# mLSTM loads and mixer stores on GpSimd's DMA queue, and a second buffer for a head's queries

## The chip, the cores and the metric

One core of a Trainium2 chip runs one program. The metric is device time in microseconds for one execution; the kernel before has a median of 1392.73 us over three runs (1391.56 to 1393.49). Five engines work side by side, each through its own instructions in order: TensorE (PE, with its weight loads as PEld), VectorE (DVE), ScalarE (ACT), GpSimd (POOL) and SyncE (SP). SP does no arithmetic here: it issues nearly all DMA transfers. POOL does arithmetic and can issue transfers too; in the profile these lie on a queue of their own kind ("software_dynamic", q0), SP's on q1 ("hardware_dynamic").

## The reference: what is computed

One transformer-like layer over two groups of rows, 1024 prompt rows and 32 sample rows, 1024 features each, all in float32:

```python
h = x * (1 + sc1) + sh1                      # adaLN, from silu(c) @ w_ada
mq, mk, mv, mo, mi, mf, fq, fk, fv, ff, gu, gv = split(h @ w_in)
hm = head_norm(mlstm(mq, mk / 8, mv, li, lf)) * g * sigmoid(mo)      # 4 heads of 64, chunked
hf = softmax_causal(fq @ fk.T / 8 + Fi - Fj) @ fv                    # 8 heads of 64, "FoX"
hg = gu * (tril(ws) @ layer_norm(gv) + bs)                           # gMLP, 4 groups
mix = concat([hm, hf, hg]) @ w_o
x = layer_norm(ALPHA * x + (1 + g1) * mix)
y = (silu(h2 @ w_gate) * (h2 @ w_up)) @ w_down                       # h2 = x * (1 + sc2) + sh2
x = layer_norm(ALPHA * x + (1 + g2) * y)
```

The mLSTM goes over the rows chunk by chunk with a matrix state C that each chunk updates; the FoX heads are causal softmax attention. New keys, values, gates and states are outputs too.

## The kernel before

**Numbers.** Each float32 product is made of three float32r products: every operand is split into a high and a low part (`whi`, `wlo`, `h1h`, `h1l`, `qkh`, `qkl`), and `gemm` issues high x high, high x low, low x high (lines 117 to 119).

**Order.** The kernel is written for a scheduler that orders each engine's instructions by a timeline simulation when the program is built. The source gives the rough order, priorities and buffer counts; the order inside an engine is the scheduler's. Tiles come from pools; a tag with one buffer means that the next tile of that tag waits until all readers of the last one are done.

**Phase one** (some 160 to 360 us in the profile) holds the projections and half of the mixing. The string `ORDER` interleaves units of the input projection (`q0` to `q7`: one FoX head's queries and keys; `k0`, `k1`, `v`, `o`: the mLSTM's; `a`: a piece of the adaLN product) with the mixers of the first 512 rows: `f0` to `f7` are `self.fox(i, ((0, 1, 2, 3),))`, `m0` to `m3` are `self.mlstm(i)`, both at a raised priority. Projections leave SBUF for DRAM scratch (`dqh`, `dql`, `dv`, `dmqk`, `dmv`, `dmo`), and the mixers load them again.

A call of `fox` issues nine loads for a head: the queries `qp` (two) and `q2` (two), the keys `k1` (two) and `k2` (two), and `v`. The tuple `foxbufs` gives the buffers of `k1`, of the queries (`qp` and `q2` together), of `k2`, of `v`, and of the transposed probabilities. In phase one it is (2, 1, 1, 2, 3). For each block of 128 queries `fox_chunk` makes the scores with two matmuls (lines 702 and 703: `qp` with `k1`, then `q2` with `k2`), the row maximum on DVE, the exponential on ACT (line 711) and the scaling on DVE (line 719); then come transposes (738), products with `v` (746, 751), and the end: ACT copies the upper half of the result to `fo` (758), DVE adds it to the lower half into `fr` (759), and `fr` is stored to `dmix`, the scratch that holds the concatenated mix, feature-major.

A call of `mlstm` handles 128 rows. It issues six loads (`mqk`, two for `mqb`, `mv`, `mo`, `mb`), all tags with one buffer; POOL clears `mqb` (525) and sets a column of `mv` (530) before their loads. ACT then makes a sigmoid of `mo` (538 to 540), POOL scales it (541), PE makes the scores (552), products (568, 573) and the new state (583), and DVE normalises (603 to 621). `to_mix` transposes the result on PE (631), ACT copies it to `mixs` (633), and a store takes it to `dmix`. `to_mix` serves the gMLP as well, with `k0=6` in place of 0.

**After phase one** the gMLP units run (`gv` with POOL's scaling in lines 353 and 354, then `gu` with `evac_gmlp`; in two of the four units POOL also makes `wlo`, line 106). The pools of phase one are closed, and the memory goes to `ph`, `pz` and `p2`: `wo_res` loads the residual (tile `z0`, seen in the profile as `mlstm_z<-xT`), `wo_mix` loads the mix from `dmix` (`wo_tmp`), and `wo` multiplies by `w_o`.

**The second half of the rows** is mixed in `mixers` (some 480 to 880 us), with another pool and `foxbufs` (2, 1, 1, 1, 2): each head takes two chunks of two tiles, woven with `mlstm(4)` to `mlstm(8)`, while the first group's feed-forward products fill PE. The rest is the second `wo` and the feed-forward of the second group.

`load` and `store` both issue on SP:

```python
    def load(self, out, in_):
        self.lastload = self.nc.sync.dma_start(out, in_)
        return self.lastload
```

## Time and profile before

| | |
|---|---|
| median of three runs | 1392.73 us (1391.56 to 1393.49) |
| the profiled execution | 1390.37 us, span 1388.5 us |
| PE busy | 1345.2 us, 97% of the span |
| DVE, ACT, POOL busy | 1034.2, 641.3, 259.1 us |
| DMA on SP's queue | 221.34 MB, 50.7% of the 16 engines |
| DMA on POOL's queue | 9.96 MB, 4.7% (all of it from line 1057, late in the kernel) |
| granted TensorE clock, mean | 0.993 |

A busy PE in these rows is not a PE at its peak: matmul ends are modelled. What tells of lost time is PE's idle time and what ended it. Idle time of the other engines costs nothing unless PE comes to wait for it.

### The profile page before, as it was taken

To read this page: it belongs to the slowest core of one execution; us is meant where nothing else is said; L and a number is where in the kernel's file an instruction comes from. 1 tells how busy PE (TensorE), PEld (TensorE's weight loads), DVE (VectorE), ACT (ScalarE), POOL (GpSimd) and SP (SyncE) were. 2 spreads that over 40 slices of the span, in tenths; PEclk is the share of its full clock that TensorE was granted. 3 is DMA by queue.
4 is the path that set the end of the run, shared out by engine and by line. 5 is a ranking of instruction groups with operands and counts; after the bars stand their busy time and mean duration, and the time that the engine had idled before them with its cause. 6 is when DMAs were issued, how large, how long until landed. Compare 5 with 4: busy or idle time off the path is not lost.

```text
span 1388.5 us, 25995 instructions
## 1 busy us (share of the span) xinstructions
PE 1345.2 (97%) x9683; PEld 1236.4 (89%) x9683; DVE 1034.2 (74%) x2214; ACT 641.3 (46%) x1261; POOL 259.1 (19%) x292
## 2 busy tenths in 40 slices
PE   7999999999999799999999999999999999999996
PEld 4899988899899778888887889899999999999996
DVE  5548656678689657777776766677898988888777
ACT  3323234444455444545544445335574544545355
POOL 0103200052157500000000000264610000000341
PEclk9999999999999899999999999999999999999998
DMA  9754577575665665444443442664497767453321
GB/s 362 266 211 134 176 242 212 187 237 149 212 205 160 180 184 182 125 131 137 133 135 86 108 127 81 195 169 134 157 229 195 216 163 214 136 175 115 101 90 65
DMA packets 136373, 233.09 MB, mean 168 GB/s; under 512 B 22564, under 2 KB 79532, under 8 KB 136248
## 3 DMA queue, kind: packets, MB, share of 16 engines
q1 hardware_dynamic: 130936, 221.34, 50.7%
q0 software_dynamic: 5168, 9.96, 4.7%
q8 instruction: 76, 1.25, 0.4%
q14 instruction: 49, 0.40, 0.1%
q10 hardware_dynamic: 144, 0.14, 0.0%
HBM read 197.50 MB, written 53.81 MB: 181 GB/s over the span
## 4 chain that ended last, share of the span: by engine, by line
PE 67%; DVE 5%; DMA 3%; ACT 1%; issue 1%; SPq 0%; POOL 0%; DVEq 0%; ACTq 0%
PE up_g L117 5%; PE up_g L118 5%; PE up_g L119 5%; PE dn_g L119 4%; PE dn_g L117 4%; PE dn_g L118 4%; PE sup_u L119 3%; PE sup_u L117 3%; PE sup_u L118 3%; PE wo_g L119 2%; PE wo_g L117 2%; PE wo_g L118 2%; PE sup_g L118 2%; PE sup_g L119 2%; PE sup_g L117 2%; PE fox_t L738 2%
## 5 line engine op out<-in xcount | busy, mean ns | idle before, releaser
L117 PE MATMUL up_g<-mlstm_ah,up_whi 128*128 128x512 f32 (+1 forms) x384 | 141.7, 369 | 4.4 <-ACT lna_tmp L981 3.3
L118 PE MATMUL up_g<-mlstm_al,up_whi 128*128 128x512 f32 (+1 forms) x384 | 142.1, 370 | 0.4 <-DVE mlstm_al L986 0.4
L119 PE MATMUL up_g<-mlstm_ah,up_wlo 128*128 128x512 f32 (+1 forms) x384 | 141.1, 368 | 0.0
L282 PE MATMUL tm_g<-tm_whi,start_h1h 128*128 128x256 f32 (+1 forms) x384 | 109.7, 287 | 1.5 <-ACT tm_mixs L633 1.5
L284 PE MATMUL tm_g<-tm_whi,start_h1l 128*128 128x256 f32 (+1 forms) x384 | 109.6, 287 | 0.0
L283 PE MATMUL tm_g<-tm_wlo,start_h1h 128*128 128x256 f32 (+1 forms) x384 | 109.5, 286 | 0.0
L117 PE MATMUL fm_g<-start_h1h,fm_whi 128*128 128x256 f32 (+2 forms) x344 | 101.7, 301 | 6.1 <-DVE fm_qkl L367 2.6
L118 PE MATMUL fm_g<-start_h1l,fm_whi 128*128 128x256 f32 (+2 forms) x344 | 100.8, 293 | 0.0
L119 PE MATMUL fm_g<-start_h1h,fm_wlo 128*128 128x256 f32 (+2 forms) x344 | 100.0, 292 | 0.0
L1105 ACT CAST sup_whi<-sup_raw 128x1024 fp32r<-128x1024 f32 x54 | 56.0, 1048 | 91.5 <-PE dn_u L118 47.9
L117 PEld LDWEIGHTS up_g<-mlstm_ah,up_whi 128*128 128x128 f32 x384 | 73.5, 192 | 16.7 <-ACT mlstm_ah L985 3.5
L118 PEld LDWEIGHTS up_g<-mlstm_al,up_whi 128*128 128x128 f32 x384 | 73.7, 192 | 12.3 <-DVE mlstm_al L986 1.5
L119 PEld LDWEIGHTS up_g<-mlstm_ah,up_wlo 128*128 128x128 f32 x384 | 73.8, 192 | 10.6
L105 ACT CAST up_whi<-up_raw 128x1024 fp32r<-128x1024 f32 x50 | 52.4, 1048 | 63.9 <-PE dn_g L118 25.1
L711 ACT ACTIVATE fox_p<-fox_s,fox_fmx 128x384 f32<-128x384 f32 (+2 forms) x96 | 55.0, 578 | 57.1 <-DVE fox_fmx L709 44.0
L282 PEld LDWEIGHTS tm_g<-tm_whi,start_h1h 128*128 128x128 f32 x384 | 72.2, 189 | 4.4 <-ACT tm_mixs L633 2.1
L117 PEld LDWEIGHTS fm_g<-start_h1h,fm_whi 128*128 128x128 f32 x344 | 64.7, 190 | 12.5 <-DVE fm_qkl L367 3.5
L1106 DVE TENSOR_TENSOR sup_wlo<-sup_raw,sup_whi 128x1024 fp32r<-128x1024 f32 x54 | 67.8, 1259 | 10.5 <-ACT sup_whi L1105 10.5
L106 DVE TENSOR_TENSOR up_wlo<-up_raw,up_whi 128x1024 fp32r<-128x1024 f32 x50 | 66.8, 1336 | 10.4 <-ACT up_whi L105 9.6
L284 PEld LDWEIGHTS tm_g<-tm_whi,start_h1l 128*128 128x128 f32 x384 | 72.2, 188 | 1.5 <-issue 1.2
L117 PE MATMUL dn_g<-up_acth,dn_whi 128*128 128x512 f32 (+2 forms) x200 | 73.5, 368 | 0.0
L118 PE MATMUL dn_g<-up_actl,dn_whi 128*128 128x512 f32 (+2 forms) x200 | 73.3, 368 | 0.0
(591 smaller groups left out, 4594.5 us busy)
## 6 DMA issues: line engine op xcount, KB each, us to landing
up_raw<-w_gu SPq DMA_DIRECT2D x50, 512.0 KB
dn_raw<-w_dn SPq DMA_DIRECT2D x28, 512.0 KB
ada_late<-w_ada SPq DMA_DIRECT2D x24, 512.0 KB
wo_raw<-w_o SPq DMA_DIRECT2D x24, 512.0 KB
sup_raw<-w_gu SPq DMA_DIRECT2D x20, 512.0 KB
start_dp<-w_gu SPq DMA_DIRECT2D x19, 512.0 KB
start_dp<-w_gu POOLq DMA_DIRECT2D x19, 512.0 KB, 7.8
sup_raw<-start_dp SPq DMA_DIRECT2D x18, 512.0 KB
```

Source lines behind the costliest of these rows:

```text
L105: nc.scalar.copy(hi[:, :w], raw[:, :w])
L106: (eng or nc.vector).tensor_tensor(lo[:, :w], raw[:, :w], f(hi[:, :w]), ALU.subtract)
L117: nc.tensor.matmul(ps, hi, xh(k), start=start and k == 0, stop=False)
L118: nc.tensor.matmul(ps, hi, xl(k), start=False, stop=False)
L119: nc.tensor.matmul(ps, lo, xh(k), start=False, stop=stop and k == n - 1)
L282: nc.tensor.matmul(ps[:, :ncol], xh, hi, start=k == 0, stop=False)
L283: nc.tensor.matmul(ps[:, :ncol], xh, lo, start=False, stop=False)
L284: nc.tensor.matmul(ps[:, :ncol], xl, hi, start=False, stop=k == 7)
L711: nc.scalar.activation(pr[:, lo:hi], banks[x][:, :hi - lo], AF.Exp, bias=mxs[:, 0:1], accum_out=sums[:, x:x + 1])
L738: nc.tensor.transpose(ps[:, c:c + P], probs[y][:, b * P:(b + 1) * P], self.ident)
L1105: nc.scalar.copy(h, x)
L1106: tt(l, x, f(h), ALU.subtract)
```

## The change

All six loads of `mlstm` are issued on GpSimd in place of SP (nine calls, 54 transfers). The mLSTM's store in `to_mix` goes to GpSimd (nine), the gMLP's stays on SP. The end of a FoX chunk adds in place into `fo`, the tile `fr` is gone, and its store goes to GpSimd (8 in phase one, 16 in `mixers`). In phase one the queries `qp` and `q2` get two buffers each.

```diff
         qk = t([P, 4, P], "mqk", 1)
-        self.load(qk[:, :, :L], self.dmqk[:, :, o:o + L])
+        self.nc.gpsimd.dma_start(qk[:, :, :L], self.dmqk[:, :, o:o + L])
         qb = t([P, 2, 2, P], "mqb")
         nc.gpsimd.memset(qb, 0.0)
         for a in range(2):
             r = slice(64 * a, 64 * a + 64)
-            self.load(qb[r, :, a, :L], self.dmqk[r, 0:2, o:o + L])
+            self.nc.gpsimd.dma_start(qb[r, :, a, :L], self.dmqk[r, 0:2, o:o + L])
         v = t([P, 4, 65], "mv1", 1)
         nc.gpsimd.memset(v[:, :, 64:65], 1.0)
-        self.load(v[:L, :, 0:64], self.dmv[:L, j, :].rearrange("p (h e) -> p h e", h=4))
+        self.nc.gpsimd.dma_start(v[:L, :, 0:64], self.dmv[:L, j, :].rearrange("p (h e) -> p h e", h=4))
         mo = t([P, 256], "mo", 1)
-        self.load(mo[:L], self.dmo[:L, j, :])
+        self.nc.gpsimd.dma_start(mo[:L], self.dmo[:L, j, :])
         mb = t([P, 4, P], "mb", 1)
-        self.load(mb[:L, :, :L], self.dM[:, j, :L].partition_broadcast(L))
+        self.nc.gpsimd.dma_start(mb[:L, :, :L], self.dM[:, j, :L].partition_broadcast(L))
...
-        self.store(self.dmix[c][:, k0:k0 + 2, o:o + L], s[:, :, :L])
+        (nc.sync if k0 else nc.gpsimd).dma_start(self.dmix[c][:, k0:k0 + 2, o:o + L], s[:, :, :L])
...
         tmp = t([64, nq], F32, "fo", 1)
-        r = t([64, nq], F32, "fr", 1)
         nc.scalar.copy(tmp[:, :nq], o[64:128, :nq])
+        r = tmp
         nc.vector.tensor_tensor(r[:, :nq], o[0:64, :nq], tmp[:, :nq], ALU.add)
         c = tiles[0] // 4
         o = tiles[0] * P - GO[c]
-        self.store(self.dmix[c][64 * (h % 2):64 * (h % 2) + 64, 2 + h // 2, o:o + nq], r[:, :nq])
+        nc.gpsimd.dma_start(self.dmix[c][64 * (h % 2):64 * (h % 2) + 64, 2 + h // 2, o:o + nq], r[:, :nq])
...
-        self.foxbufs = (2, 1, 1, 2, 3)
+        self.foxbufs = (2, 2, 1, 2, 3)
```

## The prediction

> **What bounds the kernel now.** I read the page's totals first, then the busy time by stretches, then who waited for whom on PE between 155 and 400 us, then the instructions of SP, PE, ACT and POOL around the waits found.

> ```profile
> span 1388.5 us, 25995 instructions
> PE 1345.2 (97%) x9683; PEld 1236.4 (89%) x9683; DVE 1034.2 (74%) x2214; ACT 641.3 (46%) x1261; POOL 259.1 (19%) x292
> ```

> PE is the bound; time is won only where PE stands idle. The stretches (us; busy time of PE, PEld, DVE, ACT, POOL, then the granted clock, the DMA share and GB/s) say where that is in reach of this change:

> ```profile
> 160.00:200.00 40.00, 39.77 (x328) 35.04 (x326) 17.91 (x56) 13.77 (x37) 2.04 (x4) 1.00 0.87 263
> 200.00:240.00 40.00, 38.58 (x323) 34.30 (x321) 24.06 (x58) 17.97 (x42) 2.95 (x4) 1.00 0.71 203
> 240.00:280.00 40.00, 38.35 (x320) 34.85 (x313) 25.18 (x74) 17.76 (x46) 2.09 (x4) 1.00 0.61 194
> 280.00:320.00 40.00, 38.11 (x316) 36.25 (x315) 29.86 (x92) 16.40 (x40) 16.78 (x17) 1.00 0.79 235
> 320.00:360.00 40.00, 38.95 (x329) 37.27 (x327) 35.69 (x120) 17.81 (x49) 14.39 (x15) 1.00 0.40 120
> 360.00:400.00 40.00, 35.94 (x289) 34.30 (x288) 25.06 (x54) 20.02 (x43) 8.12 (x11) 1.00 0.80 248
> 480.00:880.00 400.00, 398.93 (x2159) 331.07 (x2152) 284.64 (x610) 195.13 (x394) 9.85 (x15) 1.00 0.45 131
> ```

> Phase one (160 to 360) has 0.23 + 1.42 + 1.65 + 1.89 + 1.05 = 6.2 us of idle PE, the passage to `wo` (360 to 400) 4.1 us, and the 400 us in which the second half is mixed only 1.1 us, though most of the moved transfers lie there. What this change can win is thus a few microseconds of phase one. The waits of PE there, with total, times and longest:

> ```profile
> PE fox_s L702 <- DMA fox_qp<-start_dql: 3.3, 4, 1.6
> PE fox_s L702 <- issue: 0.7, 1, 0.7
> PE fox_s L703 <- DMA fox_k<-start_dql: 0.2, 1, 0.2
> ```

> These are the first score matmuls of a head, waiting for its queries. The one row "issue" has no releaser; I count it with them, as it stands at the same matmul. That is 4.0 us for line 702 and 0.2 us for line 703.

> **Part 1: two query buffers, and fewer transfers ahead of them on SP.** The longest of these waits, with what SP did ahead of it:

> ```profile
> 247.80 0.79 SPq L91 DMA_DIRECT2D start_dmix<-fox_fr  x1
> 248.69 0.55 SPq L87 DMA_DIRECT2D fox_qp<-start_dqh  x1
> 249.28 0.59 SPq L87 DMA_DIRECT2D fox_qp<-start_dql  x1
> 249.92 0.59 SPq L87 DMA_DIRECT2D fox_q<-start_dqh  x1
> 250.56 0.48 SPq L87 DMA_DIRECT2D fox_q<-start_dfs  x1
> 251.08 0.45 SPq L87 DMA_DIRECT2D fox_k<-start_dql  x1
> 251.57 0.48 SPq L87 DMA_DIRECT2D fox_k<-start_dfs  x1
> 253.04 0.47 PE L702 MATMUL fox_s<-fox_k,fox_qp 128*128 128x128 f32 x2 [1.65 <-DMA fox_qp<-start_dql]
> ```

> All six loads have single buffers, freed by the last head's last score matmul; they leave SP one after another, behind a head's store. With a second buffer the four query loads can go a head earlier, and only the two of `k2` still wait. Then 0.45 + 0.48 = 0.93 us of issues stand where 0.55 + 0.59 + 0.59 + 0.48 + 0.45 + 0.48 = 3.14 us stood, so `k2` leaves 2.2 us earlier, and 3.0 us with the store (0.79) gone from SP. The 4.0 us of line 702 go; the 0.2 us of line 703, late next, stay or go. I take -4.0 us, with the ends -4.2 us and 0 (if the scheduler doesn't move the loads forward, or moves the head forward with them, so that `k2` becomes the wait).

> [...]

> **Part 2: the stage from 480 to 880 us.** ACT runs in order, and a late `mo` holds what stands behind it:

> ```profile
> 739.51 0.31 SPq L87 DMA_DIRECT2D mlstm_mo<-start_dmo  x1
> 746.09 0.42 ACT L538 ACTIVATE mlstm_mo<-mlstm_mo 32x256 f32<-32x256 f32 x1 [4.76 <-DMA mlstm_mo<-start_dmo]
> 748.57 0.45 PE L702 MATMUL fox_s<-fox_k,fox_qp 128*128 128x384 f32 x1 [0.51 <-ACT fox_p L711]
> ```

> The load took 6.6 us from issue to use and cost PE 0.51 us. Whether POOL's queue brings it sooner no row shows. The ends are -1.1 us (all the idle time of the stage) and +2.5 us (five calls, each 0.51 us again); I take -0.5 us, since weights no longer stand ahead of this load on its own queue. Moving the other loads and 16 stores off SP wins nothing there: PE hides them.

> **Part 3: the store that ends phase one.** The chain of waits from 360 us on:

> ```profile
> 360.96 0.38 SPq L91 DMA_DIRECT2D start_dmix<-mlstm_mixs  x1
> 362.56 3.75 SPq L87 DMA_DIRECT2D mlstm_z<-xT  x8
> 366.35 5.20 DMA wo_tmp<-start_dmix
> ```

> The last mLSTM's store frees the memory into which the eight residual loads go, behind which the loads of the mix stand, and `wo` behind those. The store is now issued by POOL, whose only transfers so far are these (minimum, median, maximum in ns; then us to landing; then the sizes, the moved store's too):

> ```profile
> L1057 POOL DMA_DIRECT2D start_dp<-w_gu x19: 1026/1035/1533, 926.8 to 1227.2; - x19
> DMA to landing us min/median/max: 6.1/7.8/11.6
> start_dp<-w_gu POOLq DMA_DIRECT2D x19, 512.0 KB, 7.8
> start_dmix<-mlstm_mixs SPq DMA_DIRECT2D x8, 128.0 KB
> ```

> An issue takes 1.035 us on POOL against 0.38 us on SP, 0.65 us more. At the far end, a landing of 7.8 us in place of at most 1.6 us (360.96 to 362.56) is +6.2 us; but that row is of 512 KB, four times this store's 128 KB. I take +1.0 us, near the issue's difference, and charge all of it, as PE already waits in this stretch.

> **Part 4: POOL's time.** There are 54 + 9 + 24 = 87 new transfers, 87 x 1.035 = 90 us on an engine busy for 259.1 us of 1388.5. Some 36 lie in phase one (24 loads, 4 and 8 stores), 37 us, where POOL is busy for 38.3 of 200 us. On that queue stand the products of line 541, the key sums of line 368, the gMLP's scaling (353, 354) and two units' `wlo` (106). I cost that at nothing on the path: PE runs on accumulation banks filled ahead. What it costs without this cover is rival two.

> **Part 5: `fo` in place.** ACT's next copy (758) now waits for the store of the head before, where DVE's addition (759) did. The heads' stores:

> ```profile
> L91 SPq DMA_DIRECT2D start_dmix<-fox_fr x8: 452/484/949, 195.7 to 357.3; - x8
> ```

> Eight stores in 161.6 us are 23 us apart on average. Against the far landing of 7.8 us that is 0, unless POOL is held.

> **Sum.** -4.0 - 0.5 + 1.0 = -3.5 us. The profiled execution took 1390.37 us (1.9 us around its span), so it would come to 1386.9 us, a span of 1385.0. The median of the runs, 1392.73 us, lies 2.4 us over that execution; 1392.73 - 3.5 = 1389.2 us.

> **The rivals.** 0.2%, 2.8 us, is about what a measurement of this kernel can tell from no change.

> *One: the wait only changes its name.* `k2` keeps one buffer, so the scheduler may put the scores where they wait for `k2` on line 703. For: its loads are last of the six. Against: they then leave 2.2 us sooner. Parts 1 and 2 are 0 and part 3 stays: 1392.73 + 1.0 = 1393.7 us, no measurable change. It decides if the scheduler moves the scores forward by more than those 2.2 us. [...]

> *Two: POOL's queue becomes the wait, and it is slower.* The next mLSTM's loads need the last one's tiles, and the engine that issues them stands still. SP's own such waits, and POOL's work at that place:

> ```profile
> SPq L87 <- DVE mlstm_mhm L621: 12.6, 4, 4.9
> 300.31 2.40 POOL L106 TENSOR_TENSOR tm_wlo<-tm_raw,tm_whi 128x1024 fp32r<-128x1024 f32 x1 [1.30 <-ACT tm_whi L105]
> 306.67 0.52 POOL L525 MEMSET mlstm_mqb<- 128x512 f32 x1
> 308.13 0.73 POOL L353 TENSOR_TENSOR tm_traw<-tm_traw,start_rowp 128x256 f32<-128x256 f32 x1 [0.94 <-DVE tm_traw L352]
> 253.47 0.28 PE L284 MATMUL tm_g<-tm_whi,start_h1l 128*128 128x256 f32 x1
> 253.59 0.28 PE L282 MATMUL tm_g<-tm_whi,start_h1h 128*128 128x256 f32 x1
> ```

> If POOL waits up to 4.9 us for `mo`'s tile and issues for 1.0 us, `wlo` and the scaling behind it come 5.9 us late. A tile of these units is 24 matmuls, 0.12 us apart by the last two rows: 2.9 us, about what PE can bridge. Each of the three calls after the first in phase one then costs up to 5.9 - 2.9 = 3.0 us, 9.0 together; with the 3.5 us won, +5.5: 1398.2 us. Half of the calls lost, 4.5 us, gives 1393.7. For: POOL is busy for 31.2 of 80 us between 280 and 360, and some 23 transfers there add 23.8. Against: SP has long such waits only four times in the whole run, and most of POOL's work there is not urgent. It decides once a hold on POOL exceeds 2.9 us.

> [...]

> **How the numbers follow.** The forecast has 0.43, rival one 0.15, rival three 0.04, rival two 0.38: it has more than its rows alone give, because the scheduler draws up the whole order anew from POOL's costs, and an order that fits worse costs PE on the same path. So faster 0.43, same 0.19, slower 0.38. The likeliest time is 1389.2 us. Its own range is 1386.5 to 1391: the bounds of part 1 and 2 (-4.2 - 1.1 + 0.65 = -4.7) give 1388.0, and 1.5 us on each side are my estimate for the new order. The range over the cases goes down to 1385.0 and up to 1401.0, rival two with 3 us for the new order; I leave out 0.1 on each side.

> **What would show it.** Right: no DMA wait at line 702 in phase one; PE idle in 160 to 360 near 2 us in place of 6.2; query loads on SP a head ahead; POOL issues of 1.0 us, and the residual loads some 0.7 to 1 us later after the last mLSTM's copy. [...]

## The result, and the profile after

The change is slower: a median of 1401.20 us (1399.16 to 1404.78) against 1393.11 us of the kernel before, six executions each, ratio 1.0053 (1.004 to 1.0066). The profiled execution took 1402.42 us, that of the kernel before 1390.37: the two traces differ by 12 us where the medians differ by 8. The page's totals:

```profile
span 1400.3 us, 26036 instructions
PE 1353.9 (97%) x9683; PEld 1242.8 (89%) x9683; DVE 1034.3 (74%) x2214; ACT 641.7 (46%) x1261; POOL 315.1 (22%) x379
```

PE does the same 9683 matmuls and is busy for 8.7 us longer than before (1345.2); its idle time grew by only 3.1 us. In this pair of executions most of the difference isn't idle time. The stretches (busy time of PE, PEld, DVE, ACT, POOL, then the granted clock, DMA share, GB/s):

```profile
160.00:200.00 40.00, 39.35 (x318) 33.85 (x317) 18.64 (x59) 13.78 (x37) 7.19 (x11) 1.00 0.88 244
200.00:240.00 40.00, 37.88 (x306) 33.33 (x304) 22.86 (x57) 17.61 (x42) 3.27 (x5) 0.96 0.64 195
240.00:280.00 40.00, 36.99 (x287) 34.67 (x286) 20.58 (x61) 14.53 (x39) 5.63 (x9) 0.96 0.58 172
280.00:320.00 40.00, 38.09 (x313) 35.79 (x312) 25.36 (x68) 16.87 (x39) 20.63 (x24) 1.00 0.70 224
320.00:360.00 40.00, 39.64 (x335) 38.06 (x334) 35.15 (x121) 19.88 (x52) 19.78 (x27) 1.00 0.56 168
360.00:400.00 40.00, 37.61 (x314) 35.41 (x312) 25.88 (x79) 16.44 (x39) 7.61 (x12) 1.00 0.66 208
500.00:880.00 380.00, 380.00 (x2060) 315.42 (x2059) 272.92 (x585) 186.18 (x377) 33.48 (x56) 1.00 0.44 129
```

Phase one (160 to 360) is idle for 0.65 + 2.12 + 3.01 + 1.91 + 0.36 = 8.05 us, before 6.2, and the granted clock, 1.00 everywhere before, is 0.96 in two stretches. PE's waits in 155 to 400, the first four:

```profile
PE fox_s L702 <- DMA fox_q<-start_dfs: 3.0, 1, 3.0
PE fox_s L703 <- DMA fox_k<-start_dql: 2.1, 1, 2.1
PE fm_g L117 <- DVE fm_qkl L367: 1.5, 1, 1.5
PE fox_t L738 <- DVE fox_p L719: 1.4, 1, 1.4
```

Several short waits for `qp` (four, the longest 1.6) have become two long ones. No row of this stretch names `wlo` or the gMLP's scaling. The longer one, with SP ahead of it (timeline):

```profile
251.49 0.47 SPq L87 DMA_DIRECT2D fox_qp<-start_dqh  x1
252.05 0.55 SPq L87 DMA_DIRECT2D fox_qp<-start_dql  x1
252.65 1.24 SPq L87 DMA_DIRECT2D fox_k<-start_dqh  x2
253.93 0.59 SPq L87 DMA_DIRECT2D fox_q<-start_dqh  x1
254.62 0.54 SPq L87 DMA_DIRECT2D fox_k<-start_dql  x1
255.71 0.27 SPq L87 DMA_DIRECT2D fox_k<-start_dfs  x1
256.11 0.33 SPq L91 DMA_DIRECT2D start_dmo<-tm_traw  x1
256.50 0.31 SPq L87 DMA_DIRECT2D fox_q<-start_dfs  x1
258.49 0.47 PE L702 MATMUL fox_s<-fox_k,fox_qp 128*128 128x128 f32 x2 [3.01 <-DMA fox_q<-start_dfs]
```

The queries have two buffers, and yet their loads leave right before their use, now in one burst with the two loads of `k1`, the last of them behind a store. (The row puts the wait down to this last load, of `q2`, which line 702 doesn't read: it is the one that came last by the profile.) What follows the stall (three windows of 3.4 us; the figure behind the five busy times is the clock):

```profile
255.60:259.00 3.40, 0.51 (x4) 0.55 (x5) 0.00 (x0) 1.16 (x3) 0.00 (x0) 1.00 0.59 162
259.00:262.40 3.40, 3.40 (x18) 3.40 (x17) 2.48 (x8) 2.22 (x8) 0.73 (x1) 0.50 0.11 39
262.40:265.80 3.40, 3.40 (x30) 2.16 (x29) 1.18 (x5) 0.85 (x2) 0.00 (x0) 1.00 0.16 43
```

After the stall PE runs for 3.4 us at half clock: 18 matmuls where the next window has 30. PE counts as busy there, which is how busy time grows without work. Over six executions the clock averaged 0.9897, against 0.9918 of 31 of the kernel before (another job). An estimate of what that costs is 0.0021 x 1400 = 3 us, and at most that, as half-clock periods that fall on an idle PE are in the mean too (in the trace of the kernel before one starts at 469.25 us, while PE stands until 470.42). That it is a part of the loss isn't shown: e_buf below has as low a clock and loses nothing.

### The profile page after: what moved, and what is told of

Read it like the earlier page. It is cut to its first block, busy times and chain, and to the rows that moved or that the text cites. A ratio compares the mean times of both kernels' runs of the same rounds, so it can differ in the third digit from the quotient of the medians.

```text
span 1400.3 us, 26036 instructions
## 1 busy us (share of the span) xinstructions
PE 1353.9 (97%) x9683; PEld 1242.8 (89%) x9683; DVE 1034.3 (74%) x2214; ACT 641.7 (46%) x1261; POOL 315.1 (22%) x379
## 4 chain that ended last, share of the span: by engine, by line
PE 66%; DVE 4%; DMA 2%; issue 1%; ACT 1%; POOL 0%; SPq 0%; DVEq 0%; ACTq 0%; POOLq 0%
PE up_g L117 6%; PE up_g L118 6%; PE up_g L119 6%; PE dn_g L117 4%; PE dn_g L119 4%; PE dn_g L118 4%; PE sup_u L119 3%; PE sup_u L117 3%; PE sup_u L118 3%; PE wo_g L119 2%; PE wo_g L118 2%; PE wo_g L117 2%; PE sup_g L118 2%; PE sup_g L119 2%; PE sup_g L117 2%; PE fox_t L738 2%
## 5 line engine op out<-in xcount | busy, mean ns | idle before, releaser
L282 PE MATMUL tm_g<-tm_whi,start_h1h 128*128 128x256 f32 (+1 forms) x384 | 111.2, 291 | 0.0
L284 PE MATMUL tm_g<-tm_whi,start_h1l 128*128 128x256 f32 (+1 forms) x384 | 111.0, 290 | 0.0
L762 POOL DMA_DIRECT2D start_dmix<-fox_fo x24 | 13.4, 560 | 309.5 <-DVE fox_fo L759 278.2
L711 ACT ACTIVATE fox_p<-fox_s,fox_fmx 128x384 f32<-128x384 f32 (+2 forms) x96 | 55.1, 579 | 58.2 <-DVE fox_fmx L709 42.5
L105 ACT CAST up_whi<-up_raw 128x1024 fp32r<-128x1024 f32 x50 | 52.4, 1048 | 63.6 <-PE dn_g L118 23.9
L283 PEld LDWEIGHTS tm_g<-tm_wlo,start_h1h 128*128 128x128 f32 x384 | 73.8, 192 | 1.9 <-issue 1.6
L282 PEld LDWEIGHTS tm_g<-tm_whi,start_h1h 128*128 128x128 f32 x384 | 73.6, 192 | 1.8 <-issue 1.2
L284 PEld LDWEIGHTS tm_g<-tm_whi,start_h1l 128*128 128x128 f32 x384 | 73.7, 192 | 0.5 <-issue 0.4
## 6 DMA issues: line engine op xcount, KB each, us to landing
up_raw<-w_gu SPq DMA_DIRECT2D x50, 512.0 KB
dn_raw<-w_dn SPq DMA_DIRECT2D x28, 512.0 KB
ada_late<-w_ada SPq DMA_DIRECT2D x24, 512.0 KB
wo_raw<-w_o SPq DMA_DIRECT2D x24, 512.0 KB
sup_raw<-w_gu SPq DMA_DIRECT2D x20, 512.0 KB
start_dp<-w_gu SPq DMA_DIRECT2D x19, 512.0 KB
start_dp<-w_gu POOLq DMA_DIRECT2D x19, 512.0 KB, 7.5
sup_raw<-start_dp SPq DMA_DIRECT2D x18, 512.0 KB
```

The source lines that it names most:

```text
L105: nc.scalar.copy(hi[:, :w], raw[:, :w])
L282: nc.tensor.matmul(ps[:, :ncol], xh, hi, start=k == 0, stop=False)
L283: nc.tensor.matmul(ps[:, :ncol], xh, lo, start=False, stop=False)
L284: nc.tensor.matmul(ps[:, :ncol], xl, hi, start=False, stop=k == 7)
L711: nc.scalar.activation(pr[:, lo:hi], banks[x][:, :hi - lo], AF.Exp, bias=mxs[:, 0:1], accum_out=sums[:, x:x + 1])
L762: nc.gpsimd.dma_start(self.dmix[c][64 * (h % 2):64 * (h % 2) + 64, 2 + h // 2, o:o + nq], r[:, :nq])
```

## The experiments

Theories. **A**: the second query buffer makes the longer waits. **B**: the mLSTM's loads on POOL. **C**: the stores on POOL; in the form **F**, POOL stands at a head's store, its clearing of `mqb` (525) is late, and SP stands at `mqb`'s load. **Q**: any cost of POOL's queue. **D**: the scheduler's new order, drawn up for the whole program at each edit, fits the chip better or worse by chance. Each run has 4 to 12 executions, compared with 23 to 35 of the kernel before in the same job.

### The parts one by one

```diff
e_buf:        e_inplace, and foxbufs (2, 1, 1, 2, 3) -> (2, 2, 1, 2, 3)
e_loads:      mlstm: self.load(...) -> self.nc.gpsimd.dma_start(...), six loads
e_stores:     e_inplace, fox_chunk and to_mix: the stores -> nc.gpsimd (k0 = 0)
e_nobuf:      e_loads and e_stores
e_inplace:    r = tmp in place of the tile "fr"
e_buf_stores: e_buf and e_stores
e_heads:      e_inplace, and the store of fox_chunk -> nc.gpsimd
p_swap:       fox: self.load(k2[64:68]) written ahead of self.load(k2[0:64])
```

**e_buf**: 

> Only the second query buffer (with the sum in place); all transfers stay on SP. Theory A (the second buffer changes the order of the head's loads, the waits on q2 and k2 at lines 702 and 703 grow past 2 us, and each such stall is followed by some 3.4 us at half clock): the whole loss is here, 1399 to 1402 us, ratio about 1.005, granted clock under 0.993. Theory B (the mLSTM's loads on POOL's queue shift phase one): 1389 us here, as part 1 of the prediction said. Theory C (the stores through POOL): 1389 us too. Theory D (any edit makes the scheduler draw up another order, which costs or gains a few us by chance): anything from 1389 to 1401, and the costs of the parts do not add up to the whole.

**e_loads**: 

> Only the six loads of each mLSTM call are issued on POOL; one query buffer, stores on SP. Theory B: 1398 to 1402 us, ratio about 1.005, mLSTM of phase one 5 us or more later than before. Theory A and theory C: 1392 to 1394 us, ratio 0.999 to 1.001. Theory D: anything from 1389 to 1401.

**e_stores**: 

> Only the heads' stores (with the sum in place) and the mLSTM's stores of the mix are issued on POOL. Theory C: 1398 to 1402 us, with a passage to the output product that is longer by several us. Theory A and theory B: 1393 to 1395 us, the 1.0 us of part 3 being all. Theory D: anything from 1389 to 1401.

**e_nobuf**: 

> The whole change with one query buffer in place of two. Theory A: 1392 to 1395 us, the loss is gone and the clock is back at 0.993. Theories B and C: 1399 to 1402 us, as the change itself or some us worse, since the second buffer would bring its 4 us no longer. Theory D: anything from 1389 to 1401.

**e_inplace**: 

> Only the sum in place (fo and fr are one tile); the order of the instructions is that of the kernel before on every engine. All theories: no change, ratio 0.998 to 1.002. What it measures is the scatter of one and the same order from execution to execution, and in its profile which stalls come with the execution and not with the order. If it is off by more than 0.2%, the smaller ratios of the other runs mean nothing.

**e_buf_stores**: 

> Second query buffer and both kinds of stores on POOL, the mLSTM's loads on SP. Theory F (POOL, in order, stands at a head's store until DVE has made the sum; POOL's clearing of mqb behind it is late, SP stands at mqb's load, and the next head's loads behind that are late): ratio 1.004 to 1.007 as with the stores alone, and SP's wait for line 525 near 5 us as there (1.6 us before). Theory D (the scheduler's new order is good or bad by chance, the parts do not add up): anything from 0.997 to 1.008; near 1.000 speaks for D and against F. Theory A (second buffer): it lost nothing alone, so it should be as the stores alone.

**e_heads**: 

> Only the heads' stores on POOL (with the sum in place). Theory F: ratio 1.004 to 1.007, the whole loss of the stores, and SP waits for line 525 over 4 us. If the mLSTM's store of the mix is the costly one (part 3 of the prediction, mis-sized): 1.000 to 1.001 here. Theory D: anything from 0.997 to 1.008.

**p_swap**: 

> Nothing of the change: in the kernel before, the two loads of k2 are written in the other order, the same transfers on the same queue. The scheduler then draws up another order (some 370 of DVE's 2045 instructions stand elsewhere). Theory D: the time moves by several us, in either direction, as much as the change itself (ratio off 1 by 0.3% or more). Theories A, B, C and F: ratio 0.998 to 1.002, since no queue, no buffer and no wait of theirs is touched.

| run | ratio to before | 95% interval | mean clock (before) |
|---|---|---|---|
| e_inplace | 0.9997 | 0.9982 to 1.0011 | 0.9923 (0.9918) |
| e_buf | 0.9999 | 0.9984 to 1.0013 | 0.9896 (0.9915) |
| e_loads | 1.0002 | 0.9984 to 1.0019 | 0.9907 (0.9915) |
| e_heads | 1.0050 | 1.0031 to 1.0070 | 0.9892 (0.9918) |
| e_stores | 1.0048 | 1.0030 to 1.0067 | 0.9899 (0.9915) |
| e_nobuf (loads and stores) | 1.0001 | 0.9985 to 1.0017 | 0.9912 (0.9915) |
| e_buf_stores | 1.0043 | 1.0024 to 1.0061 | 0.9883 (0.9918) |
| p_swap | 1.0018 | 1.0000 to 1.0036 | 0.9907 (0.9918) |

A and B fall: neither costs anything alone. But the mechanism of A is there. PE's longest waits at the two lines in e_buf:

```profile
PE fox_s L703 <- DMA fox_k<-start_dql: 2.9, 1, 2.9
PE fox_s L702 <- DMA fox_k<-start_dqh: 1.9, 1, 1.9
```

With 0.6 us for `qp` these are 5.4 us, as in the change (5.6), and the mean clock is as low (0.9896 and 0.9897), at the time of the kernel before. So the stalls and the clock that the changed kernel's trace shows first are not shown to be its loss.

The heads' stores on POOL cost 0.5% alone, and C looks right, but the same stores cost nothing as soon as the loads go to POOL as well (e_nobuf), and cost again with the buffer on top. F falls too: SP's waits for line 525 are 5.3 us with both stores, 3.7 with the heads' alone and 1.7 with the buffer added, while the loss is the same. Costs that don't add up are what D expects. e_inplace has the order of the kernel before and its time; p_swap, which moves no transfer to any queue, has another order, and 0.18%, at the edge of its interval and under the 0.3% that D asked for.

For the place of the loss, e_inplace is the control. The score matmuls of line 702 in phase one (minimum, median, maximum ns, then first and last start) of e_inplace, of the change and of e_heads:

```profile
L702 PE MATMUL fox_s<-fox_k,fox_qp x32: 220/337/501, 170.0 to 340.8; 128*128 128x128 f32 x8, 128*128 128x256 f32 x8, 128*128 128x384 f32 x8, 128*128 128x512 f32 x8
```

```profile
L702 PE MATMUL fox_s<-fox_k,fox_qp x32: 221/336/501, 171.1 to 349.0; 128*128 128x128 f32 x8, 128*128 128x256 f32 x8, 128*128 128x384 f32 x8, 128*128 128x512 f32 x8
```

```profile
L702 PE MATMUL fox_s<-fox_k,fox_qp x32: 220/339/502, 171.3 to 347.2; 128*128 128x128 f32 x8, 128*128 128x256 f32 x8, 128*128 128x384 f32 x8, 128*128 128x512 f32 x8
```

From the first to the last they take 170.8, 177.9 and 175.9 us: in these executions the change loses 7.1 us among the eight heads, and the spans differ by 5.8 (1394.5 and 1400.3). In the second half of the rows, with 16 of the 24 heads' stores, PE has no idle time from 500 to 880 us. A single execution can't carry this further: the same matmuls take 175.9 us in the trace of e_buf and 181.2 in that of pl_full below, and the medians of both are near that of the kernel before.

### The same edit in another order, and the same order with another queue

To take D and Q apart, the program is scheduled twice. The first pass is the one whose order is wanted; in the second every instruction that stays on its engine is chained behind the one it followed (issue order, no wait), and the moved transfers find their own places (in outline):

```diff
+ order = schedule(PLAN)                     # queues and buffers of one kernel
+ for n, engine in order:                    # those of another: FINAL
+     if engine_of(real[n]) == engine:
+         tc.add_manual_dep(real[n], real[last[engine]].name, NoSync)
+         last[engine] = n
pl_full:      PLAN = before,           FINAL = the whole change
pl_heads:     PLAN = before,           FINAL = heads' stores on POOL
pl_buf:       PLAN = before,           FINAL = two query buffers
pl_rev_full:  PLAN = the whole change, FINAL = two query buffers, all on SP
pl_rev_heads: PLAN = e_heads,          FINAL = before
```

**pl_full**: 

> The whole change, in the order of the kernel before: the program is scheduled once without the change, and then built with it, every instruction that stays on its engine chained behind the one it followed before (issue order only, no wait). Only the moved transfers find their own places on POOL. Theory D (the loss is in the new order): the loss is gone, ratio 0.996 to 1.001; with the 4 us of the prediction's part 1 it would be 0.997. Theory Q (the loss is in POOL's queue: its issue time, its landing, or POOL standing at a transfer with work behind it): 1.004 to 1.007, as the change itself.

**pl_heads**: 

> Only the heads' stores on POOL, in the order of the kernel before. Theory D: ratio 0.998 to 1.002. Theory Q: 1.004 to 1.006, as the heads' stores on POOL in their own order (1.0050).

**pl_buf**: 

> Only the second query buffer, in the order of the kernel before: the loads leave SP in the old order, but the four of the queries no longer wait for the last head's scores. Theory D and the prediction's part 1: the query waits at line 702 shrink from 3 to 5 us to under 1.5, ratio 0.996 to 0.999. If the wait only changes its name (k2, line 703): 0.999 to 1.001. If stalls are merged and the clock drops more often: 1.000 to 1.002 with a granted clock under 0.991.

**pl_rev_full**: 

> The order that the scheduler drew up for the whole change, with two query buffers, but with every transfer back on SP (those find their own places on SP). Theory D: ratio 1.004 to 1.007, the loss without a single transfer on POOL ahead of 880 us. Theory Q: 0.998 to 1.001. In between (1.002 to 1.003): both.

**pl_rev_heads**: 

> The order that the scheduler drew up with the heads' stores on POOL (1.0050 there), but the stores back on SP, where the scheduler places them anew; all other instructions stand in that order on their engines. If the order alone carries the loss: 1.003 to 1.006. If it takes the order and the queue together: 1.000 to 1.002, as the old order with POOL's queue gave 1.0015. No transfer on POOL ahead of 880 us in either case, so a loss here can't come from POOL.

| run | order of | ratio to before | 95% interval |
|---|---|---|---|
| pl_full | before | 1.0014 | 0.9997 to 1.0031 |
| pl_heads | before | 1.0015 | 1.0001 to 1.0028 |
| pl_buf | before | 1.0005 | 0.9990 to 1.0019 |
| pl_rev_heads | e_heads | 1.0022 | 1.0007 to 1.0036 |
| pl_rev_full | the change | 1.0120 | 1.0103 to 1.0136 |

In the old order the whole change costs 0.14% in place of 0.53%, the heads' stores 0.15% in place of 0.50%: without the new order most of the loss is gone (1.0014 is just over D's range, and far from Q's). The order may not carry it alone: that of e_heads with its stores back on SP costs 0.22%, which lies between the two ranges that were set for it. With the queue's 0.15% that is 0.37% of the 0.50%; the rest is within the intervals. pl_rev_full can't settle it, since most of its loss is one stall, but that stall shows how order and queue hang together. PE's wait, then the timeline of DVE and SP:

```profile
PE fox_s L702 <- ACT fox_p L711: 10.1, 1, 10.1
```

```profile
184.43 0.88 DVE L547 SCALAR_TENSOR_TENSOR mlstm_mw<-mlstm_mb,start_col,start_maskbig 128x128 f32<-128x128 f32 x3 [13.58 <-DMA mlstm_mb<-start_dM]
...
180.34 5.63 SPq L535 DMA_DIRECT2D mlstm_mb<-start_dM  x2
```

The order was drawn up with `mb` loaded early by POOL (its first load left at 166.8 us in the changed kernel), and puts DVE's line 547 early. On SP that load leaves at 180.34, behind others (the row takes the loads of two calls together); DVE, in order, stands for 13.58 us, ACT behind it, PE for 10.1. An order is only as good as the arrivals it was drawn up for.

pl_buf tests part 1 of the prediction by itself. Its waits at line 702:

```profile
PE fox_s L702 <- DMA fox_qp<-start_dql: 3.8, 2, 2.9
PE fox_s L702 <- DMA fox_k<-start_dqh: 1.2, 1, 1.2
PE fox_s L702 <- ACT mlstm_mo L540: 1.0, 1, 1.0
```

They don't shrink (e_inplace, in the same order: 3.8 us for `qp`, 3 times). With SP's order kept, the query loads stand where they stood, behind other transfers; a free buffer alone moves nothing.

### Other orders for the same change

`HPA` is the bonus of the mixers' priority in phase one. Another value changes no queue and no buffer, only what the scheduler prefers:

```diff
-HPA = 200
+HPA = 400
p_hpa400: before;  full_hpa400: the whole change;  full_hpa100: the same, HPA = 100
buf_hpa400: e_buf;  nobuf_hpa400: e_nobuf
```

**p_hpa400**: 

> Nothing of the change: in the kernel before, the priority bonus of the mixers in phase one is 400 in place of 200, which gives another order (some 200 of DVE's instructions stand elsewhere). If orders differ by chance as much as the change does, 0.3% or more off 1 in either direction; if orders without POOL's queue are all alike: 0.998 to 1.002.

**full_hpa400**: 

> The whole change with the priority bonus 400 in place of 200, so the same queues and buffers in another order. If the loss hangs on the one order drawn: 0.998 to 1.003. If the queue or the stores on POOL cost it in whatever order the scheduler finds with them: 1.004 to 1.007.

**full_hpa100**: 

> The whole change with the priority bonus 100, a third order. As for 400: 0.998 to 1.003 if the loss hangs on the one order drawn, 1.004 to 1.007 if it comes with the queue in any order.

**buf_hpa400**: 

> Priority bonus 400, the second query buffer, every transfer on SP. If the buffer brings the gain of the whole change at 400 (0.9972), since there the queries are loaded ahead: 0.996 to 0.999. If it takes POOL's queue as well, or if the order at 400 was merely a lucky one: 1.000 to 1.003, as with the bonus alone (1.0022).

**nobuf_hpa400**: 

> Priority bonus 400, loads and stores on POOL, one query buffer. If the buffer brings the gain: 1.000 to 1.003. If POOL's queue brings it: 0.996 to 0.999. If it is luck of the order, either.

| ratio to before (bonus 200) | bonus 100 | bonus 200 | bonus 400 |
|---|---|---|---|
| nothing changed | | 1 | 1.0022 (1.0011 to 1.0034) |
| second buffer, all on SP | | 0.9999 | 0.9996 (0.9981 to 1.0011) |
| loads and stores on POOL | | 1.0001 | 0.9991 (0.9975 to 1.0007) |
| the whole change | 1.0060 (1.0045 to 1.0075) | 1.0053 (1.0040 to 1.0066) | **0.9972** (0.9960 to 0.9984) |

The whole change ranges from 0.28% faster to 0.60% slower with nothing but the order drawn anew. At bonus 400 it beats the kernel before at either bonus: 1392.79 us against 1396.43 (200) and 1398.17 (400), and the parts nearly add up there: against 1.0022 the buffer brings 0.26%, POOL's queue 0.31%, both 0.50%, each by its ratio to the kernel before in its own job. The bonus alone costs 0.22%, again under the 0.3% that D asked for: the two edits that change nothing but the order (p_swap is the other) cost 0.2% each. The trace of the whole change at 400 shows part 1 of the prediction as it was meant: phase one as one stretch, the waits at 702 and 703, and the timeline of the head shown above:

```profile
160.00:360.00 200.00, 196.17 (x1614) 179.90 (x1614) 126.59 (x389) 84.19 (x215) 60.13 (x78) 1.00 0.68 203
```

```profile
PE fox_s L703 <- DMA fox_k<-start_dql: 1.1, 1, 1.1
...
PE fox_s L702 <- DMA fox_qp<-start_dql: 0.5, 1, 0.5
```

```profile
242.91 0.47 SPq L87 DMA_DIRECT2D fox_qp<-start_dqh  x1
243.48 0.54 SPq L87 DMA_DIRECT2D fox_qp<-start_dql  x1
244.07 1.23 SPq L87 DMA_DIRECT2D fox_k<-start_dqh  x2
245.34 0.61 SPq L87 DMA_DIRECT2D fox_q<-start_dqh  x1
...
248.16 1.00 SPq L87 DMA_DIRECT2D fox_k<-start_dql  x1
...
249.75 0.29 SPq L87 DMA_DIRECT2D fox_q<-start_dfs  x1
...
255.71 0.50 PE L703 MATMUL fox_s<-fox_k,fox_q 68*128 68x128 f32 x2 [1.07 <-DMA fox_k<-start_dql]
```

Three of the four query loads have left 9.8 us ahead of the score matmul that waits, which waits for `k2` alone, for 1.1 us. Phase one is idle for 3.8 us, and no clock is lost in it. The second buffer isn't shown to be the reason by this trace alone: with one buffer (nobuf_hpa400) the waits for loads at the two lines are 1.2 us in all, though the queries leave late there. One order for each bonus was run, so that 400 is a better value in general isn't shown.

## Why the prediction was wrong, point by point

**Part 1 is the step that failed**: "With a second buffer the four query loads can go a head earlier". They can; whether they do is the order's. Of -4.0 us nothing came at bonus 200 (0.9999 alone, 1.0005 in the old order), and in the changed kernel the waits at 702 and 703 grew to 3.0 + 2.1 + 0.5 = 5.6 us from 4.2. The end that came true stood in the text: "0 (if the scheduler doesn't move the loads forward...)". The mechanism itself is at work where the order uses it: with all transfers on SP at bonus 400, three of the query loads leave before the last head's scores are done, and the waits for loads at the two lines fall from 3.6 us (p_hpa400) to 1.5 (buf_hpa400). The ratio improves by 0.26%, 3.6 us; not all of that is the buffer's, as a wait at line 649 also falls, from 3.7 to 0.8 us. e_loads, with 54 loads off SP and one query buffer, came out at 1.0002. In nobuf_hpa400 against p_hpa400 (0.31%) the order differs too, so that pair can't test it.

**Part 2** took -0.5 us, for a `mo` that comes sooner. Its load on POOL, and the use:

```profile
751.82 0.52 POOL L533 DMA_DIRECT2D mlstm_mo<-start_dmo  x1 [6.43 <-DVE mlstm_mhm L621]
758.24 0.42 ACT L538 ACTIVATE mlstm_mo<-mlstm_mo 32x256 f32<-32x256 f32 x1 [3.93 <-DMA mlstm_mo<-start_dmo]
```

It took 6.4 us from issue to use, where it took 6.6: no sooner. PE's idle time in 500 to 880 us (in the changed kernel, some 8 us later, PE's waits at the end of the stage before still lie behind 480) went from 0.74 us (379.26 busy of 380) to 0.00, but e_inplace, in the order of the kernel before, has 1.42. The size is no more than luck.

**Part 3** took +1.0 us for the last mLSTM's store, and read the chain wrong. In the kernel before SP waits for the landing of no store there: the residual loads (362.56) follow the gMLP's store in SP's own order, by its timeline:

```profile
362.09 0.37 SPq L91 DMA_DIRECT2D start_dmix<-tm_mixs  x1
```

In the changed kernel SP does wait (rows of POOL's and SP's timeline, and of SP's waits):

```profile
369.90 0.59 POOL L762 DMA_DIRECT2D start_dmix<-fox_fo  x1 [6.04 <-DVE fox_fo L759]
370.83 0.73 POOL L636 DMA_DIRECT2D start_dmix<-mlstm_mixs  x1 [0.35 <-ACT mlstm_mixs L633]
SPq L87 <- DMA start_dmix<-fox_fo: 2.2, 1, 2.2
372.62 3.65 SPq L87 DMA_DIRECT2D mlstm_z<-xT  x8
```

By the profile it waits 2.2 us for the last head's store, which left POOL at 369.90 and landed 2.5 us later; the mLSTM's, landing 2.4 us after 370.83, comes too late to be what these loads waited for. In the kernel before the last head's store had left at 357.32, ahead of the mLSTM's. PE pays nothing that can be seen: the 40 us that lie about the mLSTM's store as 360 to 400 did before (369.87 to 409.87) have 4.06 us of idle PE, and 360 to 400 had 4.06. So +1.0 us of PE's time was too much, and it mattered little.

**Part 4** took 1.035 us for an issue on POOL, 90 us in all. POOL's busy time grew by 56.0 us; the heads' stores and the largest loads (ns, then us to landing):

```profile
L762 POOL DMA_DIRECT2D start_dmix<-fox_fo x24: 527/548/809, 198.7 to 887.1; - x24
...
DMA to landing us min/median/max: 1.9/3.5/9.3
...
L523 POOL DMA_DIRECT2D mlstm_mqk<-start_dmqk x9: 752/776/1000, 165.3 to 739.1; - x9
```

"At nothing on the path" was right for the loads (1.0002). The landings lie between the two ends of part 3 (1.6 and 7.8 us) in the median, 3.5 us for the heads' stores and 3.2 for the mLSTM's, and the longest are beyond the far end (9.3 and 8.7).

**Part 5** was right: e_inplace is 0.9997 and leaves the order as it was.

**The sum** left out its largest term. The new order stood in it as "1.5 us on each side"; the same change, in three orders, came out between -3.9 and +8.4 us. Rival two had the clause, "the scheduler draws up the whole order anew", with 3 us for it at the far end of the range, behind a mechanism that no wait shows: from 155 to 400 us no row has PE waiting for `wlo` or the scaling. Its side and almost its time (1398.2) came out for another reason. Rival one saw the name right (line 703, 2.1 us) and took the price as nothing. No run bears out rival three (0.04): the heads' stores on POOL, nearly all issued within the time in which line 719 runs (to 869.4 us), took 0.53 to 0.81 us to issue, under the 1.026 of POOL's (larger) transfers before.

Yet `wlo` stands beside one of the rows. PE's 1.4 us for line 719 end with this scaling (POOL's and DVE's timeline):

```profile
312.87 2.37 POOL L106 TENSOR_TENSOR tm_wlo<-tm_raw,tm_whi 128x1024 fp32r<-128x1024 f32 x1
313.02 2.44 DVE L719 TENSOR_SCALAR fox_p<-fox_p,fox_fsm 128x384 f32<-128x384 f32 x1
```

The median of line 719 is 0.55 us; this one took 2.44, from just behind the start of POOL's `wlo` to just behind its end. That the one held up the other isn't shown. A scaling of 2.41 us in the middle of a `wlo` stands in full_hpa400 too, the fastest of the runs, where PE waits 1.1 us for line 719, so it isn't the loss.

**What stays open**: why the order drawn up for POOL's stores fits the chip worse, beyond the arrivals it assumes. No run here sets the scheduler's own timeline beside the trace. Where in the kernel the loss lies is open too: the traces are of single executions, and the stalls that stand out are found without a loss in e_buf. e_nobuf at 1.0001, with the same stores on POOL, is explained by D only in that D allows it.

## What to carry to other kernels

Where a scheduler draws up the order, a buffer or a queue doesn't act by itself: cost the new order as a term of its own, here up to 0.6%, more than what the edit could win. Before an edit is dropped, run it in two or three orders (another priority), and hold the old order once: that separates what the edit does from what the redraw does. And note the length of stalls, not only their sum: here the longest, over 3 us, were met or followed by 3.4 us or more at half clock in 8 of 8 cases, those of 1 to 2 us in 5 of 94.

## What the runs showed of the hardware

In the 20 profiles, between 120 and 450 us, a gap in PE's stream (from one matmul's start to the next, less the usual 0.12 us) of 1 to 2 us was met or followed by one in 5 of 94 cases, of 2 to 2.5 us in 14 of 25, of 2.5 to 3 us in 15 of 18, and a longer one in 8 of 8. Of the gaps of 2 to 3 us these are 29 of 43. What decides them isn't shown: in the changed kernel a gap of 2.13 us (from 139.78) was followed by a half-clock period, in the kernel before one of 2.03 us (from 137.68) was not.

By the windows above such a period costs (30 - 18) / 30 x 3.4 = 1.4 us, an estimate, as their matmuls are not all of one form; by the spacing of those of 256 columns, 0.12 us ahead of the stall and 0.21 behind it, it is 1.5. The scatter of one and the same program (1389.75 to 1401.32 us in 31 executions of the kernel before) goes in part with the clock (correlation -0.71; in the four other jobs -0.46 to -0.60).
